# Attention with differential heads: earlier value loads, an earlier prompt exponential, GpSimd's combination in the drain, and the first projection tile made there

## The chip, the cores and the metric

The kernel runs on one core of one Trainium2 chip. The metric is the device time of one execution in microseconds (us). A core has a TensorE (PE, matrix products, with a separate queue for its weight loads), a VectorE (DVE), a ScalarE (ACT), a GpSimd (POOL), and a SyncE (SP) that here only issues transfers. Each engine works through its own instructions in order and waits on semaphores for the others.

## The reference

One layer of a hybrid backbone for two streams that share their weights: 256 context tokens ("prompt") and 2048 latent tokens ("sample"), width 1024. Each stream does:

```python
h = rms_norm(x, norm1_g) * (1 + sc1) + sh1
q, k, v, f = project(h, w_in, q_norm_g, k_norm_g)      # 4 heads x 2 halves x 64, v 4 x 128, f 512
attn = diff_attention(q, k, v, lam)
mix = merge(attn, fourier_mix(f, w_four), subln_g, lam_init, w_out)
x = x + g1 * mix
x = x + g2 * sq_relu_mlp(rms_norm(x, norm2_g) * (1 + sc2) + sh2, w1, w2)
```

What the change touches is the attention and the merge:

```python
s = einsum('bqhmd,bkhmd->bhmqk', q, k) / sqrt(64)      # two score maps, m = 0, 1
p = softmax(s, axis=-1)
a = p[:, :, 0] - lam * p[:, :, 1]
o = einsum('bhqk,bkhe->bqhe', a, v)                    # 128 values per head
merge: concat [rms_norm(o) * (1 - lam_init) | fourier] @ w_out
```

Sample queries see 512 cached and 2048 latent keys (2560), prompt queries only the 256 prompt keys.

## The kernel before, in words

The stages follow one another: input projection (to about 480 us), Fourier mixing (to about 567), attention (to about 1321), output projection (to about 1557), MLP. Results pass between them through DRAM: `qd`, `kd`, `vd` hold queries, keys and values, `four` the Fourier result, `att` the attention result (one block of 128 tokens by 512 columns per token tile; blocks 0 and 1 are the prompt's).

**Attention.** `Head(s, h)` holds the keys `KS0`, `KS1` and the values `V` of a head (s = 0 sample, 1 prompt). Values are kept in two parts, so a product with them takes three passes (`mm3`, the lines 86 to 88); the key blocks in FULL = (4, 14) are kept whole (`vf4`, `vf14`). The sample's 2048 queries of a head are eight `Group`s of 256, numbered 0 to 7, each in two halves of 128 rows (j = 0, 1). A group's steps:

- `fill` (PE, L923): scores of 512 keys into a PSUM bank `Ss`; five banks are a row of 2560.
- `rowmax` (DVE, L928), `comb` (DVE, L931), then `exp` (ACT, L947) into `P0` (m = 0) or `P1` (m = 1), with row sums.
- `combine`: the factor lambda times the ratio of the sums (`tot`), then P0 += factor x P1, on POOL in two pieces of 1024 and 1536 columns (L969, L970). For the last group of the last head, `vcomb` = 5 gives the combination of j = 1 to DVE instead, five times 512 columns (L959).
- `tr` (PE, L979): four transposes of P0 into a bank `pts`; `ah` (ACT, L985) and `al` (DVE, L990) split it in two parts `ahs`, `als`; `mul` (PE) multiplies with the values and adds up in the left half of the bank PO (`po`). L1004 is the first matmul of a block in FULL.
- `o1` to `o6`: the sum is copied out (`oTs`, ACT), transposed into the right half of PO (PE, L1019), copied (`os`, DVE), squared (ACT), normed (`osss`; DVE, POOL L83), scaled (POOL, L1038) and stored to `att` (SP, L1039; for the last group by POOL's queue).

`Prompt` is the prompt's group of a head (names with p, as `P0p`, `op`). Its scores go to the right half of PO, `po[:, 256:512]`, and its exponentials (ACT, L1061, 128x256) read them there. There are four of them in each head, in the groups 1 to 4, one in each group.

**The order.** All steps are put in a list `ev` with a time each, sorted by it and issued under a manual schedule, so each engine's order is the order of these times. A group takes 4 T with T = 5.2, u = T/5. `AVS` = 6 is the lag, in T, between a group's score steps and its products. For head 0 the two first query loads stand at -3.03 T, its keys at -3.04 T, its values (`load_v`, L874) at 0.9 T, and the prompt's keys and values behind them.

**The banks.** `bank()` gives out PSUM: tags `S` (five banks) and `pt` (two). At the start (groups 0, 1 of head 0) and in the last group it counts with `edge` through these seven, and, at the start, PO as the eighth. In the last group the count is modulo 7.

**The output projection.** `load_wout` loads the weight in attention's last quarter. For a tile i of 128 tokens, `mix_load` loads block i of `att` (`am`, L1365) and of `four` (`mT`, L1367), `mix` transposes the block (`pmx`, L1374), copies it with a scale (`mT`, ACT) and splits it (`mh`, `ml`), `w_split` splits the weight (`woh`, `wol`), and `out_mm` multiplies step by step (k = 0 to 7). The tiles go in the order seq; s0 = 0 (the prompt's first), then s1, s2. `LASTO` holds the last group's steps o4 to o6, which are issued between the steps k = 0 to 3 and 4 to 7 of the first tile.

Of the kernel before, what the change touches and what calls it, by code (L numbers as in the profile page):

```python
# [40 lines left out]
def body(tc, a, out):  # L41
    nc = tc.nc
    ctx = ExitStack()
    with ctx:
# [795 lines left out]
        WOUT, LASTO = [], []  # L840
        with ExitStack() as c3_:
# [6 lines left out]
            kp = c3_.enter_context(tc.tile_pool(name="a_kp", bufs=1, reuse_waits="tile"))  # L848
            pS = c3_.enter_context(tc.tile_pool(name="a_ps", bufs=1, space=PSUM, reuse_waits="tile"))

            PO = pS.tile([P, 512], F32, tag="po", name="po")
            PCUT = 1024
# [30 lines left out]
            class Group:  # L883
                def __init__(self, hd, g):
                    self.hd, self.g, self.nm = hd, g, f"{hd.nm}_{g}"
                    self.S, self.mx, self.sm, self.p0, self.p1, self.tot = {}, {}, {}, {}, {}, {}
                    self.pt, self.A = {}, {}
                    self.po, self.half = None, []
                    self.nmul = 0
                    self.edge = 20 * g - 1 if hd.h == hd.s == 0 and g < 2 else None  # L890
                    self.last = hd.h == H - 1 and g == NS // 256 - 1

                    self.vcomb = 5 if self.last else 0
# [55 lines left out]
                def combine(self, j):  # L949
                    nk, tot = self.hd.nk, self.tot[j]  # L950
                    nc.vector.tensor_reduce(tot[:, 0:2], self.sm[j][:, :, 0:self.hd.nbk], axis=AX.X, op=ALU.add)
                    nc.vector.reciprocal(tot[:, 2:3], tot[:, 1:2])
                    (nc.vector if j and self.vcomb else nc.gpsimd).tensor_scalar(tot[:, 3:4], tot[:, 0:1], tot[:, 2:3], nlam, op0=ALU.mult, op1=ALU.mult)
                    nc.gpsimd.tensor_scalar(self.s0e[:, j:j + 1], tot[:, 0:1], tot[:, 0:1], EPS, op0=ALU.mult, op1=ALU.mult)
                    if j and self.vcomb:
                        for b in range(self.vcomb):
                            x = int(b * 512 >= PCUT)
                            d = self.p0[j][:, b * 512:b * 512 + 512]
                            nc.vector.scalar_tensor_tensor(d, self.p1[j, x][:, b * 512 - x * PCUT:b * 512 - x * PCUT + 512],  # L959
                                                           tot[:, 3:4], d, op0=ALU.mult, op1=ALU.add)  # L960
                        if self.vcomb == self.hd.nbk:
                            return
                    for x in range(j and self.vcomb // 2, 2):
                        lo, hi = (0, PCUT)[x], min(nk, (PCUT, 2560)[x])
                        if hi <= lo:
                            continue
                        p = self.p1[j, x][:, :hi - lo]
                        d = self.p0[j][:, lo:hi]
                        nc.gpsimd.tensor_scalar(p, p, tot[:, 3:4], 0.0, op0=ALU.mult, op1=ALU.add)  # L969
                        nc.gpsimd.tensor_add(d, d, p)  # L970

                def tr(self, kb):
                    if not kb:
                        self.edge = -1 if self.last else None
                    pt = self.bank(f"pt{self.nm}_{kb}", "pt")
                    for t in range(2):
                        for j in range(2):
                            c = (t * 2 + j) * P
                            nc.tensor.transpose(pt[:, c:c + P], self.p0[j][:, (kb + t) * P:(kb + t + 1) * P], ident)  # L979
                    self.pt[kb] = pt  # L980

                def ah(self, kb):
                    full = kb in self.hd.vf
                    t = at.tile([P, 512], F32 if full else F32R, tag="af" if full else "ah", name=f"ah{self.nm}_{kb}", bufs=2 if full else 4)
                    nc.scalar.copy(t, self.pt[kb])  # L985
                    self.A[kb] = [t]
# [6 lines left out]
                def mul(self, kb):  # L993
                    if self.po is None:
                        self.po = PO
                    A = self.A.pop(kb)
                    for t in range(2):
                        c = slice(t * 256, t * 256 + 256)
                        first = self.nmul == 0
                        self.nmul += 1  # L1000
                        last = self.nmul == self.hd.nkt
                        if len(A) == 1:
                            x = P if kb in self.half and not t else 0
                            nc.tensor.matmul(self.po[:, x:256], self.hd.vf[kb][:, t, :], A[0][:, t * 256 + x:t * 256 + 256], start=first, stop=last)  # L1004
                        else:
                            mm3(self.po[:, 0:256], self.hd.V[:, kb + t, 0, :], self.hd.V[:, kb + t, 1, :], A[0][:, c], A[1][:, c], first, last)
# [6 lines left out]
                def o1(self):  # L1013
                    self.oT = at.tile([P, 256], F32, tag="oT", name=f"oT{self.nm}")
                    nc.scalar.copy(self.oT, self.po[:, 0:256])
# [25 lines left out]
            class Prompt(Group):  # L1041
# [8 lines left out]
                def scores(self, j, m):  # L1050
                    for x in range(2):
                        nc.tensor.matmul(PO[:, 256:512], self.Q[:, x, m, j * P:j * P + P], self.hd.KS[m],
                                         start=False, stop=(x == 1), skip_group_check=True)

                def rowmax(self, j, m):
                    nc.vector.tensor_reduce(self.tl[j][:, m:m + 1], PO[:, 256:512], axis=AX.X, op=ALU.max, negate=True)

                def exp(self, j, m):
                    d = at.tile([P, 256], F32, tag=f"P{m}_1", name=f"P{m}{self.nm}_{j}")
                    (self.p1 if m else self.p0)[j] = d  # L1060
                    nc.scalar.activation(d, PO[:, 256:512], AF.Exp, bias=self.tl[j][:, m:m + 1], accum_out=self.tl[j][:, 2 + m:3 + m])  # L1061
# [19 lines left out]
                def mul(self, j):  # L1081
# [3 lines left out]
                    for t in range(2):  # L1085
                        c = slice((t * 2 + j) * P, (t * 2 + j) * P + P)
                        for l, r in ((ah[:, c], V[:, t, 0, :]), (ah[:, c], V[:, t, 1, :]), (al[:, c], V[:, t, 0, :])):
                            n += 1
                            nc.tensor.matmul(PO[:, 256 + j * P:256 + j * P + P], l, r, start=False, stop=(n == 6), skip_group_check=True)

                def o3(self):
                    self.o = self.op.tile([P, 256], F32, tag="o", name=f"o{self.nm}")
                    nc.vector.tensor_copy(self.o, PO[:, 256:512])
# [19 lines left out]

            for h in range(H):
# [4 lines left out]
                add(base + 2 * T + 0.7 if h else 0.91 * T, hp.load_k)  # L1119
                add(base + 2 * T + 0.71 if h else 0.92 * T, hp.load_v)  # L1120
# [3 lines left out]
                for j in range(2):  # L1124
                    for m in range(2):
                        for t, fn in ((0.4, gp.scores), (0.85, gp.rowmax), (3.85, gp.exp)):
                            add(G[1 + 2 * j + m] + t * u, fn, j, m)
                    add(G[2 + 2 * j] + 8 * u, gp.combine, j)
                for t, fn, *args in ((0.25, gp.tr, 0), (0.9, gp.ah), (1.4, gp.al), (15.4, gp.mul, 0), (17.0, gp.mul, 1),
                                     (20.85, gp.o3), (39.5, gp.o4), (40.2, gp.o5), (40.6, gp.o6)):  # L1130
                    add(G[5] + t * u, fn, *args)
                for g in range(hd.ng):
                    gr = Group(hd, g)
                    add(base - 4 * T + 0.6 * u if base else -3.03 * T, gr.qload)
                    for st in range(4):
# [7 lines left out]
                        if m:  # L1143
                            add(t0 + 5.9 * u, gr.combine, j)
                    kbs = list(range(0, hd.nkt, 2))
                    for q in range(4):
# [7 lines left out]
                        for n, kb in enumerate(order):  # L1154
                            add(w + tr_t[n] * u, gr.tr, kb)
                            add(w + ah_t[n] * u, gr.ah, kb)
# [6 lines left out]
                    for t, fn in ((0, gr.o1), (0.4, gr.o2), (0.75 if gr.last else 4.25, gr.o3), (8.5, gr.o4), (9.2, gr.o5), (9.6, gr.o6)):  # L1163
                        if gr.last and t > 5:
# [4 lines left out]
            add(base - 16 * T, load_wout)  # L1169
            
# [158 lines left out]
        with ExitStack() as c4, ExitStack() as c4x, ExitStack() as c4w:  # L1329
# [40 lines left out]
            def mix(i, between=None):  # L1370
                am, mT = M[i]
                pm = pp.tile([P, 4, P], F32, tag="pm", name=f"pmx{i}", bufs=1)
                for k in range(4):
                    nc.tensor.transpose(pm[:, k, :], am[:, k * P:k * P + P], ident)  # L1374
                nc.scalar.activation(mT[:, 0:4, :], pm, AF.Copy, scale=cols[:, 96:97])
# [3 lines left out]
                if between:  # L1379
                    between()  # L1380
                nc.vector.tensor_sub(ml, mT, f32(mh))
                M[i] = mh, ml
# [4 lines left out]
            def out_mm(i, hf, k0=0, k1=KD):  # L1387
# [5 lines left out]
                for k in range(k0, k1):  # L1393
                    mm3(po, mh[:, k, :], ml[:, k, :], wh[k], wl[k], k == 0, k == KD - 1)
# [528 lines left out]
```

## Time and profile before

| | |
|---|---|
| median of 3 runs | 2969.13 us (2968.26 to 2972.87) |
| the profiled execution | 2971.04 us, its span 2969.2 |
| granted TensorE clock, mean | 0.993 of full speed |
| busy share of the span | PE 98%, weight loads 85%, DVE 68%, ACT 53%, POOL 35% |
| transfers | 495.58 MB, 167 GB/s over the span |
| busy in 657 to 680 us (attention) | PE 22.34 of 23.00, POOL 21.94, ACT 20.75, DVE 19.92 |

A row of the timeline has start, duration, engine, line, operation, output<-input and the number of instructions, and in brackets the idle time of the engine before it and what ended that. A row of the waits has who waited for whom, the us in total, how often, and the longest. SPq is the queue of transfers that SP issues. A row of the windows has the busy time and number of instructions of PE, its weight loads, DVE, ACT and POOL, then the granted clock of PE, the share of time in which the DMA engines worked, and GB/s.

### The profile page before, as it was taken

Reading aid. Unit: us, or ns where it says so; the run is one execution under the profiler, and the core shown is the slowest. Engines: PE = TensorE matmul, PEld = TensorE weight load, DVE = VectorE, ACT = ScalarE, POOL = GpSimd, SP = SyncE. Lnnn points to the kernel's source line nnn. Section 1 sums busy time; section 2 is a strip of 40 time slices with the busy share of each in tenths; the row PEclk is TensorE's granted clock in tenths of the full one; section 3 lists DMA queues with packets and bytes.
Section 4 is the critical chain, followed back from the end, with each engine's and each line's share of the span. In section 5 each row is a group of like instructions: output and inputs, shape, how many; then the busy total and the mean of one; then the engine's idle time right before and its main releaser. Section 6 shows DMA issues by size and latency. Waiting matters only on the chain.

```text
span 2969.2 us, 43909 instructions
## 1 busy us (share of the span) xinstructions
PE 2906.2 (98%) x15497; PEld 2524.8 (85%) x15497; DVE 2016.8 (68%) x3381; ACT 1574.3 (53%) x3536; POOL 1032.1 (35%) x844
## 2 busy tenths in 40 slices
PE   8999999999999999989999999999999999999999
PEld 5888887778888888878889999999999888888887
DVE  6666775688888888865458778777775344345554
ACT  4333322688888889963346556556555322232221
POOL 1111112188988988942222333333332000000000
PEclk9999999999999999999999999999999999999999
DMA  7777878511121211215686667676666454445563
GB/s 275 204 194 203 229 197 250 195 59 68 51 102 37 80 65 44 85 53 167 201 251 212 219 233 233 217 241 213 219 198 229 144 176 158 138 145 175 194 215 107
DMA packets 394414, 495.58 MB, mean 167 GB/s; under 512 B 26403, under 2 KB 307056, under 8 KB 391122
## 3 DMA queue, kind: packets, MB, share of 16 engines
q1 hardware_dynamic: 386560, 477.63, 50.6%
q0 software_dynamic: 2992, 7.28, 0.8%
q10 hardware_dynamic: 4642, 7.88, 0.8%
q8 instruction: 122, 2.00, 0.3%
q14 instruction: 98, 0.80, 0.1%
HBM read 315.20 MB, written 179.57 MB: 167 GB/s over the span
## 4 chain that ended last, share of the span: by engine, by line
PE 87%; ACT 5%; DVE 4%; DMA 2%; issue 1%; POOL 0%; SPq 0%; ACTq 0%; DVEq 0%; POOLq 0%
PE Ss L923 8%; PE ps L86 8%; PE ps L87 8%; PE ps L88 8%; PE pj L86 4%; PE pj L87 4%; PE pj L88 4%; PE pts L979 4%; PE po L88 3%; PE po L86 3%; PE po L87 3%; ACT P0s L947 3%; PE pA L1549 2%; PE pA L1551 2%; PE pA L1550 2%; PE pC L1551 2%
## 5 line engine op out<-in xcount | busy, mean ns | idle before, releaser
L928 DVE TENSOR_REDUCE mxs<-Ss 128x1 f32<-128x512 f32 x637 | 415.0, 686 | 86.4 <-PE Ss L923 74.3
L1244 DVE TENSOR_TENSOR sl<-sr,sh 128x768 fp32r<-128x768 f32 x168 | 161.8, 964 | 339.8 <-ACT sh L1243 339.3
L970 POOL TENSOR_TENSOR P0s<-P0s,P1s 128x1024 f32<-128x1024 f32 x126 | 372.9, 2959 | 10.5
L1243 ACT CAST sh<-sr 128x768 fp32r<-128x768 f32 x168 | 140.1, 835 | 424.9 <-PE ps L87 423.7
L1591 POOL TENSOR_TENSOR gs<-g,g 128x384 f32<-128x384 f32 x48 | 71.8, 1496 | 482.6 <-ACT g L1561 357.9
L947 ACT ACTIVATE P1s<-Ss,mxs 128x512 f32<-128x512 f32 x318 | 215.3, 692 | 36.8 <-DVE mxs L931 36.7
L86 PE MATMUL pj<-wh,hh 128*128 128x512 f32 x576 | 229.6, 399 | 0.7 <-ACT fo L374 0.7
L87 PE MATMUL ps<-tlT,sh 128*128 128x512 f32 x585 | 229.3, 392 | 0.0
L86 PE MATMUL ps<-thT,sh 128*128 128x512 f32 x585 | 229.2, 392 | 0.0
L87 PE MATMUL pj<-wl,hh 128*128 128x512 f32 x576 | 227.7, 395 | 0.5 <-DVE wl L496 0.5
L88 PE MATMUL ps<-thT,sl 128*128 128x512 f32 x585 | 227.7, 389 | 0.0
L88 PE MATMUL pj<-wh,hl 128*128 128x512 f32 x576 | 226.3, 394 | 0.0
L947 ACT ACTIVATE P0s<-Ss,mxs 128x512 f32<-128x512 f32 x319 | 214.9, 689 | 13.2 <-DVE mxs L931 6.6
L923 PE MATMUL Ss<-KS1s,Qs 128*128 128x512 f32 x636 | 198.0, 424 | 13.1 <-ACT P0s L947 10.4
L923 PE MATMUL Ss<-KS0s,Qs 128*128 128x512 f32 x638 | 196.6, 422 | 3.3 <-ACT P1s L947 1.9
L979 PEld LDWEIGHTS pts<-ident,P0s 128*128 128x128 f32 x1280 | 159.3, 141 | 46.5 <-ACT ahs L985 3.8
L979 PE MATMUL pts<-ident,P0s 128*128 128x128 f32 x1280 | 192.7, 274 | 3.7 <-DVE als L990 2.1
L1560 ACT ACTIVATE g<-uz 128x384 f32<-128x384 f32 x144 | 75.8, 526 | 206.8 <-DVE uz L1583 176.3
L990 DVE TENSOR_TENSOR als<-pts,ahs 128x512 fp32r<-128x512 f32 x256 | 166.0, 681 | 13.1 <-ACT ahs L985 13.1
L969 POOL TENSOR_SCALAR P1s<-P1s,tots 128x1024 f32<-128x1024 f32 x126 | 169.0, 1341 | 5.7
L985 ACT CAST ahs<-pts 128x512 fp32r<-128x512 f32 x256 | 146.9, 608 | 38.3 <-PE pts L979 38.3
L86 PE MATMUL ps<-ophT,sh 128*128 128x512 f32 x423 | 165.9, 392 | 1.1 <-DVE uz L1583 1.1
(619 smaller groups left out, 8269.0 us busy)
## 6 DMA issues: line engine op xcount, KB each, us to landing
sr<-sd SPq DMA_DIRECT2D x84, 768.0 KB, 4.5
a<-in_w SPq DMA_DIRECT2D x184, 256.0 KB, 3.9
sd<-gs SPq DMA_DIRECT2D x192, 192.0 KB, 1.9
sd<-g SPq DMA_DIRECT2D x144, 192.0 KB, 4.3
wm<-in_w_mod SPq DMA_DIRECT2D x32, 512.0 KB, 5.1
Qs<-qd SPq DMA_DIRECT2D x32, 512.0 KB, 3.4
b<-in_w SPq DMA_DIRECT2D x64, 256.0 KB, 4.9
b<-tsum SPq DMA_DIRECT2D x64, 256.0 KB, 4.7
```

What stands on the lines that cost most here:

```text
L86: nc.tensor.matmul(ps, lh, rh, start=first, stop=False)
L87: nc.tensor.matmul(ps, lh, rl, start=False, stop=False)
L88: nc.tensor.matmul(ps, ll, rh, start=False, stop=last)
L923: nc.tensor.matmul(S[:, :w], self.Q[:, x, m, j * P:j * P + P], self.hd.KS[m][:, b * 512:b * 512 + w], start=(x == 0), stop=(x == 1))
L928: nc.vector.tensor_reduce(self.mx[j][:, m, b:b + 1], self.S[j, m, b], axis=AX.X, op=ALU.max)
L947: nc.scalar.activation(dst, S, AF.Exp, bias=self.mx[j][:, m, 6:7], accum_out=self.sm[j][:, m, b:b + 1])
L969: nc.gpsimd.tensor_scalar(p, p, tot[:, 3:4], 0.0, op0=ALU.mult, op1=ALU.add)
L970: nc.gpsimd.tensor_add(d, d, p)
L979: nc.tensor.transpose(pt[:, c:c + P], self.p0[j][:, (kb + t) * P:(kb + t + 1) * P], ident)
L985: nc.scalar.copy(t, self.pt[kb])
L990: nc.vector.tensor_sub(t, self.pt[kb], f32(self.A[kb][0]))
L1244: nc.vector.tensor_sub(lo, src, f32(hi))
```

## The change

- **Values ahead of the second queries.** For head 0 the query load of group 1 moves from -3.03 T to 0.6 u behind -3 T of its own base, that is from in front of `load_v` to behind it. The prompt's keys and values load at 2 T + 0.7 in head 0 too.
- **The prompt's exponential sooner.** Its time in the step goes from 3.85 u to 2.7 u, in front of the casts `ah` at 3.3 u and 3.8 u. `P1p` gets one buffer instead of two.
- **The drain's combination.** `vcomb` is gone. In the last group, j = 1, POOL combines the columns 512 to 1024 and 1024 to 2560; the first 512 are done by DVE in one instruction (`combine_v`), later in the order. `combine` stands at 4.5 u instead of 5.9 u there.
- **The drain's banks.** The seven-bank count begins in group 6 of the last head at key block 10 (`drain`) rather than with group 7's first transposes. One cast of group 6 (block 4) goes from ACT to DVE. PO becomes a bank taken anew from a pool of its own (`PRO`) each time, which lives on into the output projection and takes the transposes of its tiles.
- **The projection's first tile in the drain.** `load_wout` also loads tile 0 of `four`, into the freed weights' and values' memory; `mix0_load` (SP) loads block 0 of `att`, `mix0_tr` (PE) transposes it in front of the last group's `mul` steps, `mix0_copy` (ACT) copies it. `mix(s0)` then only splits. In the last head the prompt's o4 to o6 go forward by 5 u.
- **The entry of the projection.** `LASTO` now begins with o2, and o2, o3 are issued behind k = 0, 1, the rest behind k = 2, 3.

```diff
-                    self.vcomb = 5 if self.last else 0
+                    self.drain = hd.h == H - 1 and g == NS // 256 - 2
...
-                        n = self.edge % (7 if self.last else 8)
+                        n = self.edge % (7 if self.last or self.drain else 8)
                         if n == 7:
-                            return PO
+                            return PRO()
...
-                    (nc.vector if j and self.vcomb else nc.gpsimd).tensor_scalar(tot[:, 3:4], ...)
+                    nc.gpsimd.tensor_scalar(tot[:, 3:4], ...)
                     nc.gpsimd.tensor_scalar(self.s0e[:, j:j + 1], ...)
-                    if j and self.vcomb:
-                        for b in range(self.vcomb):
-                            ...
-                            nc.vector.scalar_tensor_tensor(d, self.p1[j, x][...], tot[:, 3:4], d, op0=ALU.mult, op1=ALU.add)
...
+                    for x in range(2):
+                        lo, hi = (512 if j and self.last else 0, PCUT)[x], min(nk, (PCUT, 2560)[x])
...
+                def combine_v(self, j):
+                    d = self.p0[j][:, 0:512]
+                    nc.vector.scalar_tensor_tensor(d, self.p1[j, 0][:, 0:512], self.tot[j][:, 3:4], d, op0=ALU.mult, op1=ALU.add)

                 def tr(self, kb):
                     if not kb:
                         self.edge = -1 if self.last else None
+                    if self.drain and kb == 10:
+                        self.edge = -1
...
-                    nc.scalar.copy(t, self.pt[kb])
+                    (nc.vector.tensor_copy if self.drain and kb == FULL[0] else nc.scalar.copy)(t, self.pt[kb])
...
+                MIX0.extend((f32(ts[0])[:, 2 * D:2 * D + 512], f32(ts[2])[:, 4 * D:5 * D].rearrange("p (k t) -> p k t", t=P)))
+                nc.sync.dma_start(MIX0[1][:, 4:8, :], four[:, 0:P].rearrange("(k p) t -> p k t", p=P))
+
+            def mix0_load():
+                nc.sync.dma_start(MIX0[0], att[0])
+
+            def mix0_tr(gr):
+                MIX0.append(gr.bank("pmx0", "pt"))
+                for k in range(4):
+                    nc.tensor.transpose(MIX0[2][:, k * P:k * P + P], MIX0[0][:, k * P:k * P + P], ident)
+
+            def mix0_copy():
+                nc.scalar.activation(MIX0[1][:, 0:4, :].rearrange("p k t -> p (k t)"), MIX0[2], AF.Copy, scale=cols[:, 96:97])
...
-                add(base + 2 * T + 0.7 if h else 0.91 * T, hp.load_k)
-                add(base + 2 * T + 0.71 if h else 0.92 * T, hp.load_v)
+                add(base + 2 * T + 0.7, hp.load_k)
+                add(base + 2 * T + 0.71, hp.load_v)
...
-                        for t, fn in ((0.4, gp.scores), (0.85, gp.rowmax), (3.85, gp.exp)):
+                        for t, fn in ((0.4, gp.scores), (0.85, gp.rowmax), (2.7, gp.exp)):
...
-                    add(G[5] + t * u, fn, *args)
+                    add(G[5] + (t - 5 if h == H - 1 and t > 30 else t) * u, fn, *args)
...
-                    add(base - 4 * T + 0.6 * u if base else -3.03 * T, gr.qload)
+                    add(base - (4 if h or g > 1 else 3) * T + 0.6 * u if base else -3.03 * T, gr.qload)
...
-                            add(t0 + 5.9 * u, gr.combine, j)
+                            add(t0 + (4.5 if gr.last and j else 5.9) * u, gr.combine, j)
+                            if gr.last and j:
+                                add(t0 + T + 5.3 * u, gr.combine_v, j)
...
+            add(base + T + 0.7 * u, mix0_load)
+            add(base + (AVS - 3) * T + 3.88 * u, mix0_tr, gr)
+            add(base + (AVS - 3) * T + 4.45 * u, mix0_copy)
...
-                mix_load(s0)
                 mix_load(s1)
                 x_load(s0)
                 x_load(s1)
-                nc.scalar.copy(WO[1][0][0], WOUT[0][:, 512:1024])
-                mix(s0, lambda: nc.vector.tensor_sub(WO[1][1][0], WOUT[0][:, 512:1024], f32(WO[1][0][0])))
-                w_split(1, 1)
-                out_mm(s0, 1, 0, 4)
-                for fn in LASTO:
+                w_split(1, 0, 1)
+                mix(s0)
+                w_split(1, 1, 4)
+                out_mm(s0, 1, 0, 2)
+                for fn in LASTO[:2]:
+                    fn()
+                w_split(1, 4)
+                out_mm(s0, 1, 2, 4)
+                for fn in LASTO[2:]:
                     fn()
```

More of the change, by code (lines that the diff above doesn't have):

```diff
@@ L1 @@
+import functools
 import math
@@ L1155, in body @@
                             add(w + tr_t[n] * u, gr.tr, kb)
-                            add(w + ah_t[n] * u, gr.ah, kb)
+                            add(w + (2.0 if gr.drain and kb == FULL[0] else ah_t[n]) * u, gr.ah, kb)
                             if al_t[n]:
@@ L1163, in body @@
                     for t, fn in ((0, gr.o1), (0.4, gr.o2), (0.75 if gr.last else 4.25, gr.o3), (8.5, gr.o4), (9.2, gr.o5), (9.6, gr.o6)):
-                        if gr.last and t > 5:
+                        if gr.last and t:
                             LASTO.append(fn)
```

59 lines of the change are left out of this document (28 added, 31 removed).

## The prediction

> **What bounds the kernel now.** I read the page's busy times and chain first.
>
> ```profile
> PE 2906.2 (98%) x15497; PEld 2524.8 (85%) x15497; DVE 2016.8 (68%) x3381; ACT 1574.3 (53%) x3536; POOL 1032.1 (35%) x844
> PE 87%; ACT 5%; DVE 4%; DMA 2%; issue 1%; POOL 0%; SPq 0%; ACTq 0%; DVEq 0%; POOLq 0%
> ```
>
> TensorE (PE) is busy 98% of the span and owns 87% of the chain that ended last. So a change is worth what PE no longer idles, or no longer spends at a low clock; work saved on another engine is worth nothing by itself. The next view is the list of waits of PE from the start of attention (567 us) to the start of the output projection: us in total, times, longest.
>
> ```profile
> PE Ss L923 <- ACT P0s L947: 11.7, 8, 6.0
> PE po L1004 <- ACT P0p L1061: 4.5, 8, 0.7
> PE po L1004 <- ACT P1p L1061: 4.5, 8, 0.6
> PE pts L979 <- ACT ahs L985: 1.6, 1, 1.6
> PE po L1019 <- ACT oTs L1015: 0.9, 2, 0.5
> ```
>
> Three places stand out: one 6.0 us wait at the start of attention, sixteen short ones on the prompt's exponentials (P0p, P1p), and those of the drain of the last two groups (ahs, oTs, and one more below). The change has a part for each. The sum is made against the profiled run, 2971.04 us (span 2969.2); the median of the three runs is 2969.13, so 1.9 us come off at the end.
>
> **Part A, the start of attention.** What holds the exponential up (start, duration, engine, line, output<-input; in brackets the idle time before it), what SP's queue does, how long the last Fourier store takes in the chain, and the sizes:
>
> ```profile
> 585.34 2.07 PE L923 MATMUL Ss<-KS1s,Qs 128*128 128x512 f32 x4 [6.04 <-ACT P0s L947]
> 584.51 0.69 ACT L947 ACTIVATE P0s<-Ss,mxs 128x512 f32<-128x512 f32 x1 [6.00 <-DMA four<-ys]
> 568.65 15.78 DMA four<-ys
> 548.06 0.81 SPq L897 DMA_DIRECT2D Qs<-qd  x2
> SPq L874 <- DMA four<-ys: 18.4, 1, 18.4
> 567.39 0.32 SPq L874 DMA_DIRECT2D Vs<-vd  x1
> Vs<-vd SPq DMA_DIRECT2D x1, 2560.0 KB
> four<-ys ACTq DMA_DIRECT2D x4, 1024.0 KB
> ```
>
> The exponential at 584.51 would have started at 578.51: it waits for the last 1 MB store of the Fourier result, whose tile its output overlaps. That store was issued at 568.65 and needed 15.78 us, because the head's values (V, 2560 KB) were issued at 567.39 and share the DMA engines with it. V came so late because SP stood 18.4 us behind its two query loads, for an earlier store of the same kind.
>
> With the change V is issued in front of the second query load. By the scheduled order it then waits only for a store that had landed by then, and goes out right behind the first query load, near 549. The second query load (512 KB) inherits the 18.4 us wait, and behind it on SP stand only loads of later groups and the prompt's K and V.
>
> ```profile
> 545.00:565.00 20.00, 20.00 (x164) 19.02 (x163) 8.26 (x21) 12.44 (x33) 0.00 (x0) 1.00 0.19 72
> 567.40:581.00 13.60, 10.97 (x38) 5.92 (x37) 11.81 (x23) 7.63 (x22) 1.71 (x3) 1.00 1.01 379
> 583.00:591.00 8.00, 5.66 (x16) 4.33 (x16) 3.94 (x7) 6.09 (x18) 5.41 (x3) 0.58 0.54 187
> 591.00:616.00 25.00, 19.65 (x74) 13.38 (x73) 17.88 (x36) 18.45 (x52) 18.19 (x12) 0.80 0.07 21
> ```
>
> These are busy times by stretch (PE, weight loads, DVE, ACT, POOL, then PE's granted clock, DMA share, GB/s). Between 545 and 565 DMA is 19% busy, so V's 2560 KB, 6.9 us at the 379 GB/s of the second row, fit there. Taken out of the stretch behind 567.4, with 0.5 MB of queries put in, they leave the last store 2.1 MB less in front: 2.1/0.379 = 5.5 us earlier, 584.43 to about 578.9. The exponential starts then at 578.5 to 578.9 and the wait is worth 5.6 to 6.0; I take 6.0. If the cover of idle DMA were not there, V would delay the stores by as much as now, and this term would be 0.
>
> Behind the 6.04 us idle the granted clock was 0.58 over 8 us and 0.80 over the next 25. PE was busy 5.66 and 19.65 there, so 0.42 x 5.66 = 2.4 and 0.20 x 19.65 = 3.9 us of it are slow clock. I count the first dip as gone with the idle time and the second as staying, because it lies behind short waits that the edit does not touch: the row gives 6.0 + 2.4 = 8.4, and I take 8, from 6 (every dip comes back) to 12.3 (none does).
>
> The Trainium skill, "TensorE: Matmul & The Clock Gate", Part 1, says the clock is halved only after an idle window of about 3.4 us; by it alone the second dip would need a long idle too, and both would go, 12.3 instead of 8. This trace speaks against it: the other seven waits on P0s in the list are 5.7 us together, 0.8 each, and the row 591 to 616 still shows 0.80.
>
> **Part B, the prompt's exponentials.** In front of each of the sixteen waits, the same picture:
>
> ```profile
> 629.00 1.09 ACT L985 CAST ahs<-pts 128x512 fp32r<-128x512 f32 x2
> 629.95 0.52 ACT L1061 ACTIVATE P0p<-po,tlp 128x256 f32<-128x256 f32 x1
> 630.61 0.92 PE L1004 MATMUL po<-ahs,vf14s 128*128 128x128 f32 x4 [0.56 <-ACT P0p L1061]
> 631.20 0.69 ACT L947 ACTIVATE P1s<-Ss,mxs 128x512 f32<-128x512 f32 x1 [0.64 <-DVE mxs L931]
> ```
>
> PE's next matmul writes the bank that the prompt's exponential reads, and that stands behind two casts on ACT. The change puts it in front of the casts: it ends 1.0 us sooner, near 629.5, and the 0.56 us wait is gone. The casts end 0.5 us later, 630.6 instead of 630.1; ACT then has its next exponential only at 631.20, so its 0.64 us of idle time takes this up. Sixteen waits are 4.5 + 4.5 = 9.0 us. With the idle time gone the cost would be the same 0.5 a time, a gain of 0 to 1. What is late next is POOL:
>
> ```profile
> 657.00:680.00 23.00, 22.34 (x145) 19.20 (x144) 19.92 (x41) 20.75 (x58) 21.94 (x20) 1.00 0.39 147
> ```
>
> In 23.0 us, about one group of queries, POOL works 21.94. With 0.56 us out of a group it has 22.44 for them, 98%: it still fits, with 0.5 to spare. I take 9.0, bounds 0 (POOL then sets the pace) and 9.0.
>
> **Part C, the drain.** The last group's second combination, five DVE instructions, goes to POOL but for its first 512 columns, group six's banks rotate over seven, and the first tile of the output projection (load, four transposes, copy) moves in front of the last multiplications.
>
> ```profile
> 1301.62 1.71 PE L979 MATMUL pts<-ident,P0s 128*128 128x128 f32 x9 [2.08 <-DVE als L990]
> 1297.56 3.40 DVE L959 SCALAR_TENSOR_TENSOR P0s<-P1s,tots,P0s 128x512 f32<-128x512 f32 x5
> 1293.00:1306.50 13.50, 11.40 (x65) 10.62 (x65) 8.53 (x17) 5.07 (x15) 3.91 (x7) 0.75 0.04 12
> 1311.24 0.37 PE L86 MATMUL po<-ahs,Vs 128*128 128x256 f32 x1
> 1320.71 0.28 PE L88 MATMUL po<-ahs,Vs 128*128 128x256 f32 x1
> 1330.83 0.48 PE L86 MATMUL po<-woh,mh 128*128 128x512 f32 x1
> ```
>
> Ahead of the last multiplications (1311.24) PE lost 1.6 and 2.1 us in waits, the second behind the DVE instructions at 1297.56, and 0.25 x 11.40 = 2.9 us to the clock. Without these 6.6 it is there at 1304.6. But there the new transposes stand, and they need row block 0 of the attention's result, which the prompt's last store completes. That store is made by POOL, behind the moved combination:
>
> ```profile
> 1290.98 3.45 POOL L970 TENSOR_TENSOR P0s<-P0s,P1s 128x1536 f32<-128x1536 f32 x1
> L970 POOL TENSOR_TENSOR P0s<-P0s,P1s 128x1536 f32<-128x1536 f32 x57 | 201.2, 3530 | 4.8
> L970 POOL TENSOR_TENSOR P0s<-P0s,P1s 128x1024 f32<-128x1024 f32 x58 | 138.8, 2394 | 4.8
> L969 POOL TENSOR_SCALAR P1s<-P1s,tots 128x1536 f32<-128x1536 f32 x58 | 90.4, 1559 | 0.0
> L969 POOL TENSOR_SCALAR P1s<-P1s,tots 128x1024 f32<-128x1024 f32 x58 | 65.1, 1123 | 5.2
> 1301.71 0.70 POOL L83 TENSOR_TENSOR osss<-osss,mhalf 128x2 f32<-128x2 f32 x1 [4.33 <-DVE osss L1032]
> 1302.52 0.72 POOL L1038 TENSOR_SCALAR os<-os,osss 128x128 f32<-128x128 f32 x2
> 1306.79 0.79 SPq L1039 DMA_DIRECT2D att<-op  x2
> att<-os SPq DMA_DIRECT2D x62, 64.0 KB, 1.6
> am<-att SPq DMA_DIRECT2D x18, 256.0 KB, 4.3
> ```
>
> POOL is free at 1294.43. A 512-wide pair is not in the trace; from 1536 to 1024 columns the prices fall by 0.44 and 1.14, so a further 512 less gives 0.69 and 1.26. With about 0.8 for two one-column instructions, and 1.56 + 3.53 for the wide pair, the sum is 7.8, some 8.1 with gaps: 1302.5. Then two small powers (0.8 each with gap) and three scalings (0.4 each): 1305.3 for the store, where before had 1306.79. It lands 1.6 us later, 1306.9; the reload goes out at once. Its 256 KB took 4.3 in the busy projection; here DMA is 4% busy, and 192 KB more than the 64 KB of 1.6 us are 0.5 us at 379 GB/s, so 2.1 to 4.3; I take 2.8, nearer the idle end: 1309.7. So PE waits 5.1 us, a new wait in place of the old ones, and I add 2.2 us of slow clock behind it (the 2.4 of part A's first dip is the nearest row). The transposes take 0.4: the multiplications start at 1312.3, 1.1 later than before. SP's reload waits there too, with only later attention stores queued behind it.
>
> What is gained comes behind the multiplications. Before, their last row (1320.71) is followed by 10 us to the fifth step of the projection's first tile (1330.83): copies, transposes, the splitting of the tile and of the weights, and four steps of the projection. Now the tile is split beside the multiplications. What is left of the 10 is four steps, 12 matmuls of 512 columns at 0.24 (twice the 20.00 us / 164 of the 256-column ones in the row of 545 to 565) = 2.9, and the wait for oTs (0.5) with as much for the transposes behind it: 3.9, so 6.1 are gained. 6.1 - 1.1 = 5.0. Bounds: 3.5 with a 4.3 us reload, 7.7 with 2.1 and without the slow clock.
>
> **The sum.** 8 + 9 + 5 = 22: 2971.04 becomes 2949.0, and the median 2947.0. A measurement of this kernel can tell about 0.2%, 5.9 us, from no change.
>
> **Rivals.**
> - POOL sets the pace (0.19). For: 98% full after part B, and PE transposes what it combines. Against: it never owned the chain (0%). If it takes part B whole, -13: 2956.
> - The clock stays full at the start (0.13), 12.3 in place of 8: 2942.7. The trace's 0.80 without long waits speaks against it; the page named above speaks for it.
> - V gains nothing (0.08): the SP queue or the stores are late still. Part A is 0: 2955. For it: SP's order alone does not show that the earlier store had landed; against, DMA's 19%.
> - The other side (0.12, of which 0.04 within 0.2%): the new wait for the reload of block 0 in the drain. Each us that it lands behind 1309.7 costs PE one. The drain itself loses from 1314.7 on, the whole from 1331.7 on, and beyond 0.2% from 1337.6 on. For: load, store and POOL's combination stand in one row behind each other and PE can pass none. Against: DMA is 4% busy there. A landing at 1339 gives 2976.
>
> **The numbers.** Forecast 0.48, the rivals 0.19, 0.13, 0.08, 0.12. Only the last is not faster: faster 0.88, same 0.04, slower 0.08. Low end: 12.3 + 9 + 7.7 = 29.0, 2940; high end: POOL's rival with part A at 6, -11: 2958. Outside lie the last rival and the ends of the bounds, under 2 in 10.
>
> **What would show it.** Right: V issued near 549, no gap over 1 us before the exponential at 578.5, no PE wait on P0p or P1p, a PE wait of some 5 us on the first tile's transposes, and the fifth projection step 4 us behind the last multiplication instead of 10. Wrong: a wait of PE or DVE on POOL in the prompt's groups (part B), a clock under 0.7 just behind 579 (part A), a landing of block 0 later than 1312 on before's axis (part C).

## The result and the profile after

| | median, us | |
|---|---|---|
| before | 2968.72 | 6 runs, 2966.15 to 2972.87 |
| changed | 2950.40 | 6 runs, 2946.64 to 2951.31 |
| ratio | 0.9934 | 95% interval 0.9922 to 0.9947, so 16 to 23 us less |

The forecast was 22.1 less (2947.0, range 2940 to 2958); by the medians it is 18.3. The profiled execution of the changed kernel took 2950.86 us, its span is 2949.1, 20.1 shorter than that of before. In its file the attention's lines stand some five further down (L923 is L928 now, L947 L952, L970 L968).

Its page: PE's busy time and the chain that ended last.

```profile
PE 2900.1 (98%) x15497; PEld 2518.1 (85%) x15497; DVE 2015.2 (68%) x3377; ACT 1570.9 (53%) x3535; POOL 1038.7 (35%) x849
PE 91%; ACT 2%; DVE 2%; DMA 2%; issue 1%; POOL 1%; SPq 0%; ACTq 0%; POOLq 0%; DVEq 0%
```

PE's share of the chain went from 87% to 91%: the same work with fewer stops. The main rows of what is left of its waits, from the end of the Fourier stage to the projection (us in total, times, longest):

```profile
PE Ss L928 <- ACT P0s L952: 5.4, 6, 1.8
PE pmx L1128 <- DMA wout<-att: 5.1, 1, 5.1
PE Ss L928 <- ACT P1s L952: 2.4, 2, 2.0
PE po L1024 <- ACT oTs L1020: 0.4, 1, 0.4
```

The waits on P0p and P1p are gone, those on P0s have lost their 6.0, and one new wait has come, on the reload of block 0 of the attention's result.

**The ledger.** An instruction that occurs equally often in both traces can be paired by its number. DVE's combination of the row maxima does (128 times), and so does a norm in the projection. The difference of the starts, after minus before, says where the time went:

| place (start before, us) | offset | this stretch |
|---|---|---|
| first maximum of attention (571.5) | +2.0 | +2.0 |
| the first of group 2 (614.6) | -6.1 | -8.1 |
| the first of the last group (1270.7) | -15.7 | -9.6 |
| norm of the projection's first tile (1353.4) | -20.3 | -4.6 |
| last step of the MLP (2956.0) | -20.2 | +0.2 |

Set against the terms of the forecast, 8, 9 and 5, the three parts come out at 8.1, 9.6 and 4.6. What the forecast had no term for is the first line.

**The start of attention.** SP's queue, the last Fourier store in the chain, and the stretches that answer to those of before:

```profile
550.52 0.37 SPq L880 DMA_DIRECT2D Vs<-vd  x1
569.37 0.37 SPq L886 DMA_DIRECT2D vf4s<-vs  x1
570.69 7.21 DMA four<-ys
580.42 0.73 ACT L952 ACTIVATE P0s<-Ss,mxs 128x512 f32<-128x512 f32 x1
581.00:589.00 8.00, 7.71 (x24) 3.27 (x22) 7.57 (x16) 7.75 (x25) 7.49 (x6) 1.00 0.31 116
589.00:614.00 25.00, 19.45 (x90) 14.16 (x90) 18.85 (x38) 19.39 (x53) 23.32 (x17) 0.86 0.06 21
```

V goes out at 550.5 instead of 567.4, the last store takes 7.2 us instead of 15.8, and the exponential at 580.42 has no idle time in front of it. The clock just behind is 1.00 (0.58 before); in the 25 us that follow it is 0.86 (0.80 before).

**The prompt's exponential** now stands ahead of the two casts, and PE's matmul (the third row) carries no wait. The fourth row is POOL's window, the fifth the only thing that POOL waits for in the groups:

```profile
622.86 0.49 ACT L1066 ACTIVATE P0p<-po,tlp 128x256 f32<-128x256 f32 x1
623.30 1.09 ACT L990 CAST ahs<-pts 128x512 fp32r<-128x512 f32 x2
623.78 0.82 PE L1009 MATMUL po<-ahs,vf14s 128*128 128x128 f32 x4
657.00:680.00 23.00, 22.94 (x149) 19.76 (x147) 21.20 (x41) 21.19 (x61) 21.22 (x17) 1.00 0.42 155
POOL tots L959 <- DVE tots L958: 29.6, 25, 1.7
```

**The drain.**

```profile
1280.27 1.30 POOL L968 TENSOR_TENSOR P0s<-P0s,P1s 128x512 f32<-128x512 f32 x1
1287.15 0.73 POOL L84 TENSOR_TENSOR osss<-osss,mhalf 128x2 f32<-128x2 f32 x1
1289.82 0.86 SPq L1044 DMA_DIRECT2D att<-op  x2
1291.43 0.32 SPq L1123 DMA_DIRECT2D wout<-att  x1
1293.93 1.12 PE L1128 MATMUL pmx<-ident,wout 128*128 128x128 f32 x4 [5.12 <-DMA wout<-att]
1295.00:1300.00 5.00, 5.00 (x24) 4.82 (x23) 1.11 (x2) 1.92 (x4) 0.00 (x0) 0.50 0.02 3
1306.61 0.28 PE L89 MATMUL po<-ahs,Vs 128*128 128x256 f32 x1
1310.49 0.48 PE L87 MATMUL po<-woh,mh 128*128 128x512 f32 x1
```

POOL's queue runs without a gap from the last combination to the prompt's scaling, then come the store, 1.6 us later the reload, 2.5 us later PE. The clock is 0.50 behind the wait. From the last multiplication (1306.61) to the projection's fifth step (1310.49) it is 3.9 us, where it was 10.1.

### The profile page after: what moved, and what is told of

The parts are those of the page before. It is cut to its first block, busy times and chain, and to the rows that moved or that the text cites. A ratio compares the mean times of both kernels' runs of the same rounds, so it can differ in the third digit from the quotient of the medians.

```text
span 2949.1 us, 43913 instructions
## 1 busy us (share of the span) xinstructions
PE 2900.1 (98%) x15497; PEld 2518.1 (85%) x15497; DVE 2015.2 (68%) x3377; ACT 1570.9 (53%) x3535; POOL 1038.7 (35%) x849
## 4 chain that ended last, share of the span: by engine, by line
PE 91%; ACT 2%; DVE 2%; DMA 2%; issue 1%; POOL 1%; SPq 0%; ACTq 0%; POOLq 0%; DVEq 0%
PE Ss L928 10%; PE ps L88 8%; PE ps L87 8%; PE ps L89 8%; PE pts L983 5%; PE pj L87 4%; PE pj L88 4%; PE pj L89 4%; PE po L87 4%; PE po L89 4%; PE po L88 4%; PE pA L1577 2%; PE pB L1577 2%; PE pC L1579 2%; PE pB L1578 2%; PE pC L1577 2%
## 5 line engine op out<-in xcount | busy, mean ns | idle before, releaser
L968 POOL TENSOR_TENSOR P0s<-P0s,P1s 128x1024 f32<-128x1024 f32 (+2 forms) x128 | 377.0, 2945 | 10.7
L952 ACT ACTIVATE P1s<-Ss,mxs 128x512 f32<-128x512 f32 x318 | 215.5, 694 | 36.7 <-DVE mxs L936 36.3
L952 ACT ACTIVATE P0s<-Ss,mxs 128x512 f32<-128x512 f32 x319 | 215.0, 690 | 6.3 <-DVE mxs L936 5.7
L928 PE MATMUL Ss<-KS1s,Qs 128*128 128x512 f32 x636 | 197.0, 422 | 6.8 <-ACT P0s L952 4.1
L928 PE MATMUL Ss<-KS0s,Qs 128*128 128x512 f32 x638 | 197.0, 421 | 3.9 <-ACT P1s L952 2.4
L967 POOL TENSOR_SCALAR P1s<-P1s,tots 128x1024 f32<-128x1024 f32 (+2 forms) x128 | 172.1, 1345 | 5.8
L89 PE MATMUL ps<-ophT,sl 128*128 128x512 f32 x423 | 165.7, 392 | 0.0
```

The source lines that it names most:

```text
L89: nc.tensor.matmul(ps, ll, rh, start=False, stop=last)
L928: nc.tensor.matmul(S[:, :w], self.Q[:, x, m, j * P:j * P + P], self.hd.KS[m][:, b * 512:b * 512 + w], start=(x == 0), stop=(x == 1))
L952: nc.scalar.activation(dst, S, AF.Exp, bias=self.mx[j][:, m, 6:7], accum_out=self.sm[j][:, m, b:b + 1])
```

## The experiments

**Each part alone.** Values first, on the kernel before:

```diff
-                add(base + 2 * T + 0.7 if h else 0.91 * T, hp.load_k)
-                add(base + 2 * T + 0.71 if h else 0.92 * T, hp.load_v)
+                add(base + 2 * T + 0.7, hp.load_k)
+                add(base + 2 * T + 0.71, hp.load_v)
...
-                    add(base - 4 * T + 0.6 * u if base else -3.03 * T, gr.qload)
+                    add(base - (4 if h or g > 1 else 3) * T + 0.6 * u if base else -3.03 * T, gr.qload)
```

> The kernel before with the load order of head 0 alone changed (values in front of the second queries, prompt's keys and values later). Theory: the last Fourier store no longer shares the DMA engines with the values, so the exponential that waited 6.0 us for it starts at once, and the first low-clock stretch behind it goes too: 8 us less, 2961 beside 2969. Rival 1, the clock stays low at its new place: 6 us less, 2963. Rival 2, loading 2.5 MB of values at 550 us delays the Fourier stage's own loads and stores: the Fourier stage ends about 2 us later (in the changed kernel its last store was issued 2.0 us later than before) and the gain is 6 us.

Measured: 2964.92 beside 2971.17, ratio 0.9978 (0.9969 to 0.9986), 6.3 us less. In the ledger the first 43 us of attention (571 to 614) are 7.3 us shorter, but the stage begins 2.2 us late, so that 5.1 are left at group 2. The exponential behind the last store starts without a wait. The interval, 4 to 9 us, holds the theory's 8 and the 6 of both rivals, so the trace has to tell them apart. Against rival 1, the clock is 1.00 from 581 to 589; it falls later, to 0.86 from 589 to 614. Against rival 2, the 2.2 us are there before V goes out; the numbers are below, under the sum.

The prompt's exponential, on the kernel before:

```diff
-                        for t, fn in ((0.4, gp.scores), (0.85, gp.rowmax), (3.85, gp.exp)):
+                        for t, fn in ((0.4, gp.scores), (0.85, gp.rowmax), (2.7, gp.exp)):
```

> The kernel before with the prompt's exponential alone moved from 3.85 u to 2.7 u. Theory: the sixteen waits of PE on P0p and P1p are gone, 9 us less (the traces of the changed kernel show 9.7 across the four heads), 2960 beside 2969, and PE waits for POOL nowhere in the groups. Rival, POOL sets the pace: 0 to 5 us less, with waits of PE on POOL or of DVE casts on transposes in the groups 1 to 4 of each head.

Measured: 2959.68 beside 2971.17, ratio 0.9961 (0.9949 to 0.9974), 11.5 us less, more than the theory's 9, though the interval, 8 to 15 us, holds it. Its list of waits has no P0p and no P1p, and none on POOL. By the ledger the groups give 9.6, as in the changed kernel, and 3.4 more come from the drain, whose code is that of before. The two long waits there are the same to 0.1 us (their total, times, longest), the clock is not; the two windows of the kernel before stand below those of this one:

```profile
PE pts L979 <- DVE als L990: 2.0, 1, 2.0
PE pts L979 <- ACT ahs L985: 1.6, 1, 1.6
1280.00:1290.00 10.00, 6.21 (x48) 5.53 (x46) 6.10 (x12) 5.83 (x18) 4.85 (x3) 1.00 0.01 2
1290.00:1302.00 12.00, 11.69 (x92) 10.82 (x93) 6.09 (x12) 7.04 (x18) 2.83 (x6) 1.00 0.08 23
```

```profile
1290.00:1300.00 10.00, 7.61 (x46) 7.07 (x46) 4.76 (x10) 5.60 (x16) 4.61 (x3) 0.83 0.01 2
1300.00:1312.00 12.00, 10.34 (x70) 9.57 (x71) 5.36 (x11) 5.41 (x13) 2.83 (x6) 0.86 0.08 22
```

0.17 x 7.61 + 0.14 x 10.34 = 2.7 us of slow clock in the one and none in the other, behind waits of 1.6 and 2.0 us in both. What decides this is in the last section.

The drain alone, that is the changed kernel with the other two edits taken back (the diffs above, reversed; `P1p` keeps its one buffer):

> The changed kernel with the load order of head 0 and the prompt's exponential put back: only the drain, its banks and the first projection tile differ from before. Theory: PE waits about 5 us on the reload of block 0 and loses some 2 us of clock behind it, and the entry of the projection still gains 6: 4.5 to 5 us less in all, 2964 beside 2969. Rival: the parts lean on each other, the drain gains nothing by itself (2968 to 2969) and the rest of the gain of the whole change, 18 us, is due to the other two parts.

Measured: 2966.78 beside 2971.17, ratio 0.9981 (0.9972 to 0.9990), 4.4 us less, and 4.7 in the ledger. It has the new wait on its own:

```profile
PE pmx L1128 <- DMA wout<-att: 5.3, 1, 5.3
```

The three alone make 6.3 + 11.5 + 4.4 = 22.2 us, each known to some 3 us either way, beside 18.3 (16 to 23) for all together. The parts do not lean on each other in any way that these runs can tell.

**Why the last store was late: bytes or queue.** Before, V stood behind the second queries on SP. Here it stays behind them and goes out later still:

```diff
-                add(base - 14 * T + 0.7 if h else 0.9 * T, hd.load_v)
+                add(base - 14 * T + 0.7 if h else 2.9 * T, hd.load_v)
```

> The kernel before with the values of head 0 loaded later (2.9 T in place of 0.9 T), in their old order behind the second queries: they go out behind the Fourier stores. Theory, the last store was late because 2.5 MB of values shared the DMA engines with it: with them behind it the store lands some 6 us sooner, the exponential no longer waits, and the gain is that of the load order alone, 7 to 8 us in the trace behind the start of attention, 2964 beside 2971, although SP's queue is as before. Rival: it is SP's order that counts, SP standing 18 us at a wait; then nothing is gained, 2971. A late load of values would show as a wait of PE's first product on them near 615 us.

Measured: 2964.42 beside 2969.46, ratio 0.9981 (0.9972 to 0.9990), 5.0 us less. The chain of waits, SP and a window:

```profile
568.98 7.16 DMA four<-ys
572.07 1.20 SPq L874 DMA_DIRECT2D Vs<-vd  x1
588.00:613.00 25.00, 19.46 (x106) 14.69 (x107) 20.06 (x40) 21.10 (x59) 24.04 (x18) 1.00 0.06 21
```

The store takes 7.2 us as in the changed kernel, with SP at its 18.4 us wait as before and V issued 3 us behind the store instead of 20 in front. So it is the 2.5 MB issued 1.3 us ahead of the store that cost the 6 us, not SP's standing still; the rival falls. PE's first products on V do not wait for it. The window shows that the second dip can be absent too: PE is busy as long as in the changed kernel's row of 589 to 614 (19.46 and 19.45), at 1.00 instead of 0.86. In this profiled execution the start of attention is 10.2 us shorter, not 8.

**How far the exponential has to move.** Half as far, between the two casts:

```diff
-                        for t, fn in ((0.4, gp.scores), (0.85, gp.rowmax), (3.85, gp.exp)):
+                        for t, fn in ((0.4, gp.scores), (0.85, gp.rowmax), (3.5, gp.exp)):
```

> The kernel before with the prompt's exponential alone moved only between the two casts (3.5 u), half as far as in the change. Theory, the wait of 0.56 us was one cast's length (0.54): it goes nearly whole, sixteen times 0.5, 8 to 9 us less within attention, 2962 beside 2971. Rival: the exponential ends too late for PE's matmul still and half of the wait stays, 4 to 5 us less, 2966.

Measured: 2962.17 beside 2969.46, ratio 0.9974 (0.9965 to 0.9983), 7.3 us less; the ledger gives 7.8 within the groups. Of the sixteen waits two are left in the list, 0.2 us each:

```profile
PE po L1004 <- ACT P0p L1061: 0.2, 1, 0.2
PE po L1004 <- ACT P1p L1061: 0.2, 1, 0.2
```

So one cast's length covers most of it, as expected, at the low end of the 8 to 9 us: each of the sixteen steps is 0.5 us shorter, with both casts behind the exponential 0.6.

**The new wait in the drain.** Three versions of the changed kernel attack it. First, the transposes behind the last multiplications:

```diff
-            add(base + (AVS - 3) * T + 3.88 * u, mix0_tr, gr)
-            add(base + (AVS - 3) * T + 4.45 * u, mix0_copy)
+            add(base + AVS * T + 4.5 * u, mix0_tr, gr)
+            add(base + AVS * T + 5.5 * u, mix0_copy)
```

> The changed kernel with the four transposes of the first projection tile and their copy behind the last multiplications instead of in front of them; the reload stays where it is. Theory: the 5.1 us wait and the 2.2 us of slow clock behind it go, but the transposes, copy and split of the tile stand on the path again between the last multiplication and the projection's first matmul, about 3 us: 4 us below the changed kernel, 2946. Rival: with the wait gone another one in the drain takes its place and the time stays near 2950.

Measured: 2948.05, ratio 0.9924 (0.9910 to 0.9938) to before. Against the changed kernel's 0.9934 that is 3 us, where the theory had 4, and the ledger's drain is 7.5 instead of 4.6, 2.9 better. The wait has moved, not gone: the tile's split is now on the path.

```profile
1302.71 0.47 PE L87 MATMUL po<-woh,mh 128*128 128x512 f32 x1 [2.27 <-DVE mh L1405]
```

Second, the prompt's last norm, scaling and store ahead of POOL's last combination, the reload right behind that store, and two DVE instructions instead of one:

```diff
-                    add(G[5] + (t - 5 if h == H - 1 and t > 30 else t) * u, fn, *args)
+                    add(G[5] + ({39.5: 24.9, 40.2: 26.0, 40.6: 26.4}[t] if h == H - 1 and t > 30 else t) * u, fn, *args)
...
-            add(base + T + 0.7 * u, mix0_load)
+            add(base - T + 1.5 * u, mix0_load)
...
-                        lo, hi = (512 if j and self.last else 0, PCUT)[x], min(nk, (PCUT, 2560)[x])
+                        lo, hi = (PCUT if j and self.last else 0, PCUT)[x], min(nk, (PCUT, 2560)[x])
...
-                    d = self.p0[j][:, 0:512]
-                    nc.vector.scalar_tensor_tensor(d, self.p1[j, 0][:, 0:512], self.tot[j][:, 3:4], d, op0=ALU.mult, op1=ALU.add)
+                    for b in range(2):
+                        d = self.p0[j][:, b * 512:b * 512 + 512]
+                        nc.vector.scalar_tensor_tensor(d, self.p1[j, 0][:, b * 512:b * 512 + 512], self.tot[j][:, 3:4], d, op0=ALU.mult, op1=ALU.add)
```

> The changed kernel with the last prompt's norm, scaling and store in front of POOL's last combination, the reload right behind that store, and DVE combining the first 1024 columns of the last half (two instructions) in place of 512. Theory: the wait of 5.1 us of the first tile's transposes was the reload standing behind POOL's combination; here block 0 is there some 6 us sooner, the wait and the slow clock behind it go, and the time is 5 to 7 us below the changed kernel, 2944 beside 2950.4. Rival: other stalls take its place (the last transposes wait for POOL's or DVE's combination), and the gain is under 2 us, 2949 to 2950.

Measured: 2944.29 beside 2971.17 before, ratio 0.9910 (0.9897 to 0.9924), some 6 us below the changed kernel, as the theory had it. Third, the same without the last edit, POOL still combining from column 512:

> The changed kernel with the last prompt's norm, scaling and store in front of POOL's last combination and the reload right behind, but POOL still combining from column 512 on. Theory: the wait for block 0 goes as in the version with DVE's second instruction, but POOL's last combination ends some 1.5 us later, at 1288.7 on the changed kernel's axis, and the transposes that stood at 1287.8 wait about 0.9 us for it: 1 to 2 us slower than that version, 2945 to 2946. Rival: the second DVE instruction is what paid, and the time is near the changed kernel's (2949 to 2951).

Measured: 2943.66 beside 2969.46, ratio 0.9913 (0.9899 to 0.9926). POOL, SP, PE and the window:

```profile
1278.86 0.72 POOL L1043 TENSOR_SCALAR op<-op,ossp 128x128 f32<-128x128 f32 x2
1280.85 0.32 SPq L1123 DMA_DIRECT2D wout<-att  x1
1288.11 0.55 PE L983 MATMUL pts<-ident,P0s 128*128 128x128 f32 x3 [0.26 <-POOL P0s L968]
1285.00:1295.00 10.00, 9.71 (x81) 9.13 (x80) 4.15 (x8) 5.40 (x14) 5.85 (x7) 1.00 0.06 15
```

The reload goes out at 1280.85 instead of 1291.43, no wait on it is left, and the clock stays at 1.00. The 0.9 us that POOL's longer queue was to cost are 0.26. The second DVE instruction brings nothing that the two times show; in the ledgers the drain gains 12.8 us with it and 12.3 without.

The changed kernel and this version once more, on one chip:

> The changed kernel once more, beside the version with the early store on the same chip. Theory: its reload wait of 5 us and the slow clock behind it are in every execution, so it stays 5 to 8 us above that version. Rival: the difference between the two was one of sessions and clock dips, and they come within 3 us of each other.

> The version with the last prompt's store in front of POOL's last combination, once more, beside the changed kernel on the same chip. Theory: 5 to 8 us below it, 25 to 27 us below the kernel before; nothing but the drain differs in the traces. Rival: within 3 us of it.

Measured: 2951.12 and 2943.99 beside 2971.22, ratios 0.9931 (0.9917 to 0.9945) and 0.9913 (0.9899 to 0.9927). The version is 7.1 us below the changed kernel by the medians; in the ledgers the drain brings 4.5 and 12.3 us, a difference of 7.8, and 5.2 of it is the wait for block 0 in this execution. This version beats both kernels.

## Why the prediction was right, and where its terms were off

**Part A, 8 us: right in size and cause.** 6.0 for the wait came as worked out: the store's 15.8 us became 7.2, and the run with V behind the store shows that it was V's bytes. The store is 8.6 us shorter where the sum had 5.5; the wait could give no more than its 6.0, as the exponential was not ready before 578.5 in any case. Two details were different. The second queries did not inherit SP's 18 us wait directly, the small value blocks did (vf4s, at 569.37); nothing in the list of waits shows a price for it. And the clock: the forecast let the first dip go and kept the second, which the profiled execution shows (1.00, then 0.86), but it was luck in part. Eight traces are without the 6 us wait, seven with V early and the one with V late. Six of them have 6.8 us at half clock in the 25 us that follow, and their stretch is 6.9 to 8.1 us shorter than before's; two have none (the changed kernel's second profile and V late), and gain 10.1 and 10.2. A term of 8 with 12 as the upper bound was the right form; a single number for a dip was not. The Trainium skill ("TensorE: Matmul & The Clock Gate", Part 1) has the clock halve after an idle window of some 3.4 us, and calls that window free-running, so that the same kernel can meet it at another phase. The length and the phase agree with these traces, that the window must be idle does not: half clock stood behind windows of 3.41 us in which PE was busy for 1.39 us in the drain of before, and for up to 2.03 elsewhere (rows in the last section).

**Part B, 9 us: right.** The ledger has 9.6 to 10.1 for the groups in all seven traces with the exponential at 2.7 u, a little over the term and its upper bound of 9.0. That bound is the waits alone. Behind a wait PE's four products also take 0.57 us to the next row (630.61 to 631.18), without one 0.47: 0.1 a time, and 1.6 over sixteen, would cover the rest, by this estimate. The rival that POOL sets the pace did not come: its list of waits still shows 29.6 us in which it waited for DVE (37.7 before), and 21.22 busy us of 23. The forecast of 98% had taken POOL's fullest window of before, 21.94, which holds three instructions more than the one shown here; the changed kernel's window with as many, 634 to 657, has 21.68, so POOL has little to spare but does not lead.

**Part C, 5 us: right in size, and nearly term by term.** POOL's path was 512-wide pieces of 0.71 and 1.30 us (0.69 and 1.26 forecast), though its last 1536-wide scaling took 2.09 where the sum had 1.56; the store to reload to landing took 1.6 + 2.5 us (1.6 + 2.8); the wait 5.1 (5.1), the slow clock behind it 0.50 x 5.00 = 2.5 in the window shown (2.2); the way from the last multiplication to the projection's fifth step 3.9 (3.9). What the ledger finds is 4.6. It is a little flattered, as the drain of the profiled execution of before was itself at a low clock: with its old code it was 0.6 to 3.4 us shorter in the four other executions that have it. So the 2.9 us of clock, which the sum booked as a cost of the old code, were in part chance. The upper bound of 7.7 adds up to 7.9 from its own terms (5.0 + 0.7 + 2.2), which changes nothing.

**The sum, 22 against 18.3.** In the traces the three parts make 22.3, and the +2.0 with which attention begins leaves 20.2 at the end. The other 1.9 us lie in the choice of executions: the profiled one of before is 2.3 us above the median of its six, that of the changed kernel 0.5. Of the +2.0, paired products of PE show 0.5 from 300 us on and 1.5 more between 484 and 505, ahead of every instruction that the change moves. PE waits there for the Fourier stage's constants,

```profile
PE pabE L87 <- DMA c<-in_c: 3.6, 1, 3.6
```

(3.2 before), and the clock in 480 to 500 is 0.83 (0.91). With the load order of before the offset at the start of attention was -0.6, +1.0, +0.3 and +1.8 in four executions; with the values moved +2.2, +1.4, +0.9, +2.2, +1.6 and +1.1 in six. The means differ, 0.6 and 1.6, but not for the reason that rival 2 of the first experiment gives. V goes out at 549.4 to 550.7, and from the product that stands at 548.0 in before to the one at 566.0 the offset changes by at most 0.02 us in each of the seven traces with V early (2.03 and 2.03 in the changed kernel's). Loading V early thus delays nothing in the Fourier stage that PE shows; the offset is older, and what sets it in each execution stays open.

**The rival on the other side** was the right place to look: block 0 landed at 1293.9, on before's axis (15.7 us later there) 1309.6, the forecast's 1309.7. It costs 7.8 us of what the drain could bring, without turning the sign, and a change of four times in the order takes it away.

## What to carry to other kernels

Price an early load by what it shares the DMA engines with, not by where it stands in its queue: 2.5 MB beside a 1 MB store cost 6 us on the path, 20 us earlier or 3 us later they cost nothing that the runs show. When a step is moved forward onto an engine that cannot pass it, follow what it needs back through every queue: here a 5 us wait of PE was made by a store that stood behind a combination it has nothing to do with. And compare two traces stretch by stretch with paired instructions before comparing sums, because slow clock and waits in unchanged stretches can be as large as the part under study.

## What the runs showed of the hardware that was not expected

The granted clock behind short waits varies between executions of the same code: the drain of before ran at 0.83 and 0.86 in one profile and at 1.00 in another, behind the same waits of 1.6 and 2.0 us, worth 2.7 us; the 25 us behind 589 (588 in the run with V late) ran at 0.86 or at 1.00 with 19.45 us of PE work in each, worth up to 0.14 x 19.45 = 2.7 us again.

What decides can be seen when the windows are cut where the clock changes. In each of the twelve traces, from 60 us on, the granted clock is 1.00 or 0.50 and changes only on a grid with a step of 3.41 us, and where the steps fall differs from execution to execution. Here are two steps of the drain of before, then two of the run with the prompt's exponential alone moved, both around the 1.6 us wait:

```profile
1289.44:1292.86 3.42, 1.39 (x12) 0.91 (x10) 0.20 (x1) 3.42 (x11) 3.34 (x2) 1.00 0.00 0
1292.86:1296.27 3.41, 3.41 (x17) 3.41 (x18) 1.38 (x2) 0.96 (x2) 1.57 (x1) 0.50 0.03 7
1279.01:1282.42 3.41, 2.00 (x16) 1.52 (x15) 0.87 (x2) 3.41 (x12) 3.33 (x3) 1.00 0.00 0
1282.42:1285.83 3.41, 2.80 (x25) 2.80 (x26) 2.00 (x5) 1.91 (x5) 2.31 (x2) 1.00 0.03 7
```

In the first the whole wait falls into one step, PE is busy for 1.39 us of it, and the next step runs at half clock. In the second the border of two steps cuts the wait, PE is busy for 2.00 and 2.80 us, and the clock stays full. Of all steps at full clock in the twelve traces, but for the first 60 and the last 20 us, the 33 in which PE was busy for less than 1.59 us were all followed by half clock; of the 45 with 1.59 to 2.04 us, 22 were; with more, none was. So the same short wait costs up to 1.7 us, half of one step, or nothing, by where the grid cuts it.

No part of the change sets where the steps fall, and a sum of terms cannot reach it. The clock goes with the spread between runs: of the changed kernel's first six, the two at a mean clock of 0.997 took 2946.64 and 2947.54 us, the four at 0.994 or 0.995 took 2950.28 to 2951.31.
